# The shared expert and the router of a second transformer block, as products of split operands

## The chip, the core and the metric

The kernel runs on one core of a Trainium2 chip. Such a core has a matrix engine (TensorE, PE in the profile; its weight loads are PEld), a vector engine (VectorE, DVE), an activation engine (ScalarE, ACT), a general engine (GpSimd, POOL) and a queue engine (SyncE, SP). Each follows its own list of instructions in order; semaphores make one wait for another. SP and ACT also issue DMA transfers; those queues are SPq and ACTq in the profile. The metric is the time of one execution on the device in microseconds (us); less is better.

## The reference

Two transformer blocks, 512 tokens, model width 1024, all in float32. The second block is the one that matters here. It ends in

```python
    x = x + gate_m * hybrid_mixer(h, ...)                       # last product of the mixer: merged @ w_out
    h = rms_norm(x, g_ffn_norm[l]) * (1.0 + scale_f) + shift_f
    x = x + gate_f * moe_ffn(h, w_router, b_router, w_exp_gate, w_exp_up, w_exp_down,
                             w_sh_gate, w_sh_up, w_sh_down)
return rms_norm(x, g_final)
```

and `moe_ffn` is

```python
    scores = jax.nn.sigmoid(xf @ w_router)                      # 64 experts
    ...                                                         # 4 of 8 groups, then 6 experts per token
    shared = (jax.nn.silu(xf @ w_sh_gate) * (xf @ w_sh_up)) @ w_sh_down    # 1024 -> 256 -> 1024, every token
    return shared + routed
```

The rows `gate_m`, `scale_f`, `shift_f`, `gate_f` (1024 values each, one batch) come from a conditioning vector and are computed earlier in the kernel. The 64 routed experts have 3 MB of weights each.

## The kernel before

A tile is 128 partitions by so many elements; the 512 tokens are four tiles, t0 to t3. `xres` is the residual stream, tokens on partitions.

**Split operands.** Most dense products are made from operands in two parts. `hi` is the value copied to the type float32r, `lo` is the value minus `hi`, also float32r; `mm3` (lines 108 to 110) adds `hi*hi`, `lo*hi` and `hi*lo` in one PSUM bank. For weights `Kernel.weights` does it: it loads a chunk `w` of 128x1024 by SP's queue, ACT makes `wh` (line 136), and DVE or POOL makes `wl` (line 137). Both halves have two buffers, so a chunk's `wh` waits until PE is done with the chunk two before. The shared expert, the router and the routed experts use plain float32 products.

**Output projection (`finish` in `phase_c`).** `merged @ w_out` is made in two column halves, g = 0 and g = 1, each with four PSUM banks (one per token tile) and four weight chunks of 24 matmuls, 96 matmuls in all. Chunks 0 and 1 go over all four tiles; then each tile takes chunks 2 and 3 and is finished. Then DVE multiplies the bank with the gate row `gm` (line 1805) and adds it to `xres` (line 1806). The banks come from the pool `pj`, which has four:

```python
    def pbank(self, name="pbank"):
        return self.pj.tile([128, 512], F32, tag="p", name=name)
```

so the first matmul of g = 1 on t0 waits for the `xres` addition of g = 0 on t0.

**Head (`phase_d`).** Its loads are issued while `finish` runs: on ACT's queue the rows `scale_f` and `shift_f` (tile `rows`), `g_ffn_norm` and `gm` (the two halves of tile `gmr`), and, in the place of `g_ffn_norm` once that is used, the router's weights; on SP's queue the shared expert's weights (`sg` twice, `sd`) and the first expert weights. `rows` is completed by DVE at line 1852. For each tile, `head(t)` computes the norm, `logits(t)` makes `h`, writes it to DRAM (`hD`, from which the experts gather), transposes it (`xt`, 8 transposes), copies it to SBUF (`hT`) and multiplies with the router's weights (`lg`).

**Rest of the head (`rest_d`).** A sigmoid on the logits, the choice of experts on DVE (ending in `Ab`), counts, ranks and positions by small matmuls (`cnt`, `key`, `perm`, `pos`, `posT`, `posR`, `GT`, `Gr`, `ce`), then for each of the first units the chosen token numbers (`bc` on PE, `st`, `jk`, `ii` on DVE), the gather of their rows by POOL (`xg`) and of their gates (`gg`). Beside it PE computes the shared expert: `g` and `u` (64 instructions of 256 columns each), the hidden row on ACT and DVE, two transposes `hT`, `y` (32 instructions of 512 columns). DVE multiplies each `y` bank with the row `gf` (line 1005), and POOL adds it to `xres` (line 1974).

**Expert loop (`Moe.run`).** Units of routed experts follow, each: transposes `xT` of the gathered rows, `g`, `u`, `y`, and a scatter product `sc` added to `xres`. Weights come by SP's queue into 18 slots (15 + 2 + 1) shared with the head's own tiles; `O1` and `O2` say which group of slots the next tile takes, `F0` and `F1` how many units are fetched ahead, and `LP`, `RP` are priorities. The order on each engine is fixed at build time by a list scheduler that goes by program order, priorities and its own estimates.

Of the kernel before, what the change touches and what calls it, by code (L numbers as in the profile page):

```python
# [18 lines left out]
S, D = 512, 1024  # L19
# [35 lines left out]
class K:  # L55
# [611 lines left out]
LAST = 2  # L667

# [77 lines left out]
class Moe:  # L746
# [33 lines left out]
    def slot(self, shape, dt, name, hold=False, after=None):  # L780
# [713 lines left out]
def phase_c(k, rctx, rp, rows):  # L1494
# [293 lines left out]
    def finish(gm, done):  # L1788
        for g in range(2):
            gs_ = slice(512 * g, 512 * g + 512)  # L1790
            banks = [k.pbank("wo") for _ in range(NT)]
            ws = [k.weights(pw, [(I["w_out_2"][0], 512 * g, 512 * g + 512)], 2 * h, 2, 512, eng=nc.vector if WV[1] else None) for h in range(4)]
# [8 lines left out]
            for t in range(NT):  # L1801
# [3 lines left out]
                nc.vector.tensor_mul(b, b, gm[:, gs_])  # L1805
# [7 lines left out]
F0, F1 = 2, 3  # L1813
# [3 lines left out]
O1 = [0] * 3 + [1] * 2 + [0] * 12  # L1817
O2 = [0] * 3 + [1] * 2 + [2] + [0] * 12
# [6 lines left out]
def phase_d(k, out):  # L1825
# [19 lines left out]
    perm = f.tile([1, E], I32, name="perm")  # L1845
    rows_ = moe.slot([128, 2, D], F32, "rows")
# [7 lines left out]
    wr = gmr[:, 1, :KD * E].rearrange("p (k n) -> p k n", k=KD)  # L1854
    nc.scalar.dma_start(wr, I["w_router_2"][0].rearrange("(p k) n -> p k n", p=128))
# [23 lines left out]
    def logits(t):  # L1879
        lb, rs = lbs[0], rss[t]  # L1880
        ts = slice(t * 128, (t + 1) * 128)
        h, hT = h4[t // 2][:, t % 2], hTs[t]
        nc.vector.scalar_tensor_tensor(h, k.xres[:, t], rs, gs, op0=ALU.mult, op1=ALU.mult)
        nc.vector.tensor_add(h, h, sh)
        nc.scalar.dma_start(moe.hD[ts], h)
        for c in range(2):
# [3 lines left out]
            nc.scalar.activation(hT[:, 4 * c:4 * c + 4], b.rearrange("p (k s) -> p k s", k=4), AF.Copy)  # L1890
        for kk in range(KD):
            nc.tensor.matmul(lb[:, t * E:(t + 1) * E], lhsT=hT[:, kk], rhs=wr[:, kk], start=kk == 0, stop=kk == KD - 1)

    def rest():
        for t in range(NT - LL, NT):
            with tc.high_priority(LP):
                logits(t)
        moe.rooms()
        moe.work()
        rest_d(k, out, moe, lbs[0], br, f, perm, hTs, shared, ctx)  # L1900
# [3 lines left out]
def rest_d(k, out, moe, lb, br, f, perm, hTs, shared, ctx):  # L1904
# [62 lines left out]
    ws = [(128, shared)]  # L1967
    hTx = moe.m.tile([128, NT, 2, 128], F32, tag="xT", name="hTx", bufs=1)
    for t in range(NT):
        moe.hidden(hTs[t], ws, None, k.pbank, hT=hTx[:, t])  # L1970
    for t in range(NT):
        def add(h, b):
            xs = k.xres[:, t, h * 512:(h + 1) * 512]
            nc.gpsimd.tensor_add(xs, xs, moe.scaled(h, b, moe.m.tile([128, 512], F32, tag="yl", name="ysh", bufs=2)))
        moe.down(hTx[:, t], ws, add)
# [73 lines left out]
```

## Time and profile before

| | us |
|---|---|
| median of three runs (1662.69, 1664.47, 1668.43) | 1664.47 |
| the profiled execution | 1666.99 |
| its span | 1664.9 |
| PE busy in the span | 1543.6 |
| DVE / ACT / POOL busy | 968.7 / 540.6 / 341.9 |

The profiled execution lies 2.5 us above the median; 2.1 us of it lie outside the span. PE is busy for 93% of the span, and the chain of work that ended last runs on PE for 47% of the span and little on any other engine. Times in the text below are us from the start of the span. The second block's `finish` runs from 1009 to 1061, the head from there to 1126, the expert loop from 1126 to about 1650.

In a timeline each line is: start, duration, engine and source line, operation, output <- inputs, shapes, and in square brackets how long the engine was idle before and what released it. In groups of instructions it is: busy us, mean ns of one, then the idle time before them and its releaser. PEclk is the clock granted to PE as a share of 2.4 GHz.

### The profile page before, as it was taken

To read this page: it belongs to the slowest core of one execution; us is meant where nothing else is said; L and a number is where in the kernel's file an instruction comes from. 1 tells how busy PE (TensorE), PEld (TensorE's weight loads), DVE (VectorE), ACT (ScalarE), POOL (GpSimd) and SP (SyncE) were. 2 spreads that over 40 slices of the span, in tenths; PEclk is the share of its full clock that TensorE was granted. 3 is DMA by queue.
4 is the path that set the end of the run, shared out by engine and by line. 5 is a ranking of instruction groups with operands and counts; after the bars stand their busy time and mean duration, and the time that the engine had idled before them with its cause. 6 is when DMAs were issued, how large, how long until landed. Compare 5 with 4: busy or idle time off the path is not lost.

```text
span 1664.9 us, 28632 instructions
## 1 busy us (share of the span) xinstructions
PE 1543.6 (93%) x10917; PEld 1038.3 (62%) x10917; DVE 968.7 (58%) x2217; ACT 540.6 (32%) x1087; POOL 341.9 (21%) x285
## 2 busy tenths in 40 slices
PE   5899999988999877899999998999999999999996
PEld 4665557765565446675657776865666665665653
DVE  3599536853554347537554535555665666656656
ACT  4534676331211124555552222301211112112112
POOL 2324451012101103331104442022101111111000
PEclk9999999987999997999999999999999999999998
DMA  6443326368999963233005836758999999999961
GB/s 188 147 164 117 105 82 234 133 216 309 418 417 416 418 264 106 72 90 106 26 1 188 257 118 222 305 197 350 378 416 385 398 411 420 424 417 422 420 288 64
DMA packets 104783, 420.78 MB, mean 253 GB/s; under 512 B 23508, under 2 KB 30138, under 8 KB 67268
## 3 DMA queue, kind: packets, MB, share of 16 engines
q1 hardware_dynamic: 82880, 388.20, 60.7%
q0 software_dynamic: 9968, 19.04, 3.2%
q10 hardware_dynamic: 11796, 11.68, 2.2%
q8 instruction: 87, 1.43, 0.3%
q14 instruction: 52, 0.43, 0.1%
HBM read 419.99 MB, written 9.21 MB: 258 GB/s over the span
## 4 chain that ended last, share of the span: by engine, by line
PE 47%; DVE 4%; DMA 3%; POOL 1%; ACT 1%; issue 1%; SPq 0%; DVEq 0%; ACTq 0%; POOLq 0%
PE g L973 8%; PE u L973 7%; PE sc L1051 7%; PE y L997 7%; PE qk L1671 2%; PE ob L1699 2%; DMA mw<-in_w_mod_dram 2%; PE xT L938 2%; PE pt L110 2%; PE pt L109 2%; PE pt L108 2%; PE pt L1691 1%; DVE macc L1400 1%; DMA w<-in_w_in_dram 1%; PE wo L109 1%
## 5 line engine op out<-in xcount | busy, mean ns | idle before, releaser
L137 POOL TENSOR_TENSOR wl<-w,wh 128x1024 fp32r<-128x1024 f32 (+4 forms) x72 | 167.1, 2323 | 370.2 <-ACT wh L136 348.1
L1052 DVE TENSOR_TENSOR xres<-xres,sc 128x512 f32<-128x512 f32 x368 | 224.4, 681 | 3.4 <-PE sc L1051 1.0
L973 PE MATMUL u<-wu,xT 128*32 128x256 f32 (+2 forms) x2240 | 176.0, 388 | 11.2 <-DMA wu<-in_w_exp_up_dram 9.4
L973 PE MATMUL g<-wg,xT 128*32 128x256 f32 (+2 forms) x2240 | 173.6, 383 | 1.0 <-DMA wg<-in_w_exp_gate_dram 0.9
L915 POOL DMA_INDIRECT xg<-hD,ii x46 | 46.1, 1002 | 599.0 <-issue 500.7
L997 PE MATMUL y<-wd,hT 128*32 128x512 f32 (+2 forms) x1120 | 167.6, 596 | 0.0
L979 DVE SCALAR_TENSOR_TENSOR hid<-u,gc,hid 128x256 f32<-128x256 f32 x46 | 22.3, 484 | 232.8 <-PE u L973 227.7
L973 PEld LDWEIGHTS g<-wg,xT 128*32 128x32 f32 (+2 forms) x2240 | 99.2, 119 | 87.5 <-issue 31.5
L1051 PE MATMUL sc<-yh,st 128*128 128x512 f32 x368 | 152.2, 416 | 0.0
L973 PEld LDWEIGHTS u<-wu,xT 128*32 128x32 f32 (+2 forms) x2240 | 105.1, 121 | 73.0 <-DMA wu<-in_w_exp_up_dram 12.0
L136 ACT ACTIVATE wh<-w 128x1024 fp32r<-128x1024 f32 (+4 forms) x88 | 89.9, 1022 | 186.8 <-PE pt L109 85.3
L1051 PE MATMUL sc<-yl,st 128*128 128x512 f32 x368 | 144.4, 395 | 0.1
L987 ACT ACTIVATE hT<-hT 128x256 f32<-128x256 f32 x46 | 17.7, 385 | 299.5 <-PE hT L984 299.5
L116 ACT ACTIVATE yh<-y 128x512 fp32r<-128x512 f32 x92 | 54.9, 597 | 163.0 <-DVE y L1005 129.1
L108 PE MATMUL pr<-wh,xh 128*128 128x512 f32 (+2 forms) x256 | 101.9, 402 | 5.9 <-ACT wh L136 5.4
L109 PE MATMUL pr<-wl,xh 128*128 128x512 f32 (+2 forms) x256 | 101.2, 397 | 5.9 <-POOL wl L137 5.9
L997 PEld LDWEIGHTS y<-wd,hT 128*32 128x32 f32 (+2 forms) x1120 | 46.6, 118 | 90.7 <-issue 88.0
L117 DVE TENSOR_TENSOR yl<-y,yh 128x512 fp32r<-128x512 f32 x92 | 63.6, 692 | 67.1 <-ACT yh L116 66.7
L110 PE MATMUL pr<-wh,xl 128*128 128x512 f32 (+2 forms) x256 | 100.2, 395 | 0.2 <-DVE xl L117 0.2
L110 PE MATMUL pt<-xh,wl 128*128 128x512 f32 x224 | 90.1, 402 | 2.9 <-POOL wl L137 2.9
L108 PE MATMUL pt<-xh,wh 128*128 128x512 f32 x224 | 91.1, 407 | 0.5 <-ACT la L1570 0.3
L109 PE MATMUL pt<-xl,wh 128*128 128x512 f32 x224 | 89.8, 401 | 0.0
(532 smaller groups left out, 2802.6 us busy)
## 6 DMA issues: line engine op xcount, KB each, us to landing
wg<-in_w_exp_gate_dram SPq DMA_DIRECT2D x96, 1024.0 KB, 14.3
wu<-in_w_exp_up_dram SPq DMA_DIRECT2D x96, 1024.0 KB, 11.8
wd<-in_w_exp_down_dram SPq DMA_DIRECT2D x96, 1024.0 KB, 13.0
w<-in_w_in_dram SPq DMA_DIRECT2D x52, 512.0 KB, 3.7
mw<-in_w_mod_dram SPq DMA_DIRECT2D x32, 512.0 KB, 4.7
mw<-in_w_mod_dram SPq DMA_DIRECT2D x8, 1024.0 KB, 5.8
w<-in_w_out_dram SPq DMA_DIRECT2D x16, 512.0 KB, 4.5
brs<-brd ACTq DMA_DIRECT2D x1, 2560.0 KB
```

The costliest lines, as they stand in the source:

```text
L108: nc.tensor.matmul(out, lhsT=lh, rhs=rh, start=first, stop=False)
L109: nc.tensor.matmul(out, lhsT=lh, rhs=rl, start=False, stop=False)
L110: nc.tensor.matmul(out, lhsT=ll, rhs=rh, start=False, stop=last)
L116: hi = nc.scalar.activation(dh, src, AF.Copy)
L117: lo = nc.vector.tensor_sub(dl, src, dh.bitcast(F32))
L136: nc.scalar.activation(wh[:, :, :c], w[:, :, :c], AF.Copy)
L137: (eng or nc.gpsimd).tensor_sub(wl[:, :, :c], w[:, :, :c], wh[:, :, :c].bitcast(F32))
L915: self.gathered = nc.gpsimd.indirect_dma_start(out=x, out_offset=None, in_=src, in_offset=bass.IndirectOffsetOnAxis(ap=ii[:, :1], axis=0), ...
L973: nc.tensor.matmul(b[sl], lhsT=xT[:, kk, sl], rhs=g[h][:, kk], start=kk == 0, stop=kk == KD - 1)
L997: nc.tensor.matmul(b[sl], lhsT=hT[:, j, sl], rhs=d[:, j, h * 512:(h + 1) * 512], start=j == 0, stop=j == 1)
L1051: nc.tensor.matmul(b, lhsT=st[:, ts], rhs=y[h][i], start=i == 0, stop=i == 1)
L1052: nc.vector.tensor_add(self.acc[:, t, hs], self.acc[:, t, hs], b)
```

## The change

Five edits, all in the second block:

1. For g = 1 of the output projection, `gm` is multiplied into the weights (four times 128x1024 on DVE, new argument `times`), not onto the four banks.
2. The shared expert is made with `mm3`. Its weights are loaded as four 512 KB pieces (`sgu`, gate and up side by side) and `sd`, `gf` is multiplied into `sd`, and they are split (ACT `sgh` twice, `sdh`; DVE `sgl` twice, `sdl`); `y` is added to `xres` by DVE straight from the bank.
3. The router's weights stand as `hi` and `lo` side by side in 128 columns (`mid`); the transposed `h` is split too (`hh`, `hl`). Each pair of token tiles gets 16 matmuls of 256 columns. The bank holds two halves of rows that must be added: ACT copies it, and four float32 matmuls with a matrix `sum2` (two identities) add the halves and transpose (`lo`).
4. The first two units of the expert loop are prepared at high priority (`RUN`).
5. `F0` goes from 2 to 1, another fetch of 2 units follows, and `O1`, `O2` are changed for the new use of slots.

The core of the diff, cut:

```diff
-    def weights(self, pool, segs, k0, nk, width, wb=2, eng=None):
+    def weights(self, pool, segs, k0, nk, width, wb=2, eng=None, times=None):
...
+            if times is not None:
+                nc.vector.tensor_mul(w, w, times[:, None, :].to_broadcast([128, nk, width]))
...
+RUN = {32: 0, 64: 400}
...
-        for u in range(2):
-            self.pick(u)
-        self.prep(0)
-        with self.k.tc.issue_after(self.indexed.ins):
-            self.prep(1)
+        with self.k.tc.high_priority(RUN[self.E]):
+            for u in range(2):
+                self.pick(u)
+            self.prep(0)
+            with self.k.tc.issue_after(self.indexed.ins):
+                self.prep(1)
...
-            ws = [k.weights(pw, [(I["w_out_2"][0], 512 * g, 512 * g + 512)], 2 * h, 2, 512, eng=nc.vector if WV[1] else None) for h in range(4)]
+            ws = [k.weights(pw, [(I["w_out_2"][0], 512 * g, 512 * g + 512)], 2 * h, 2, 512, eng=nc.vector if WV[1] else None,
+                            times=gm[:, gs_] if g else None) for h in range(4)]
...
-                nc.vector.tensor_mul(b, b, gm[:, gs_])
+                if not g:
+                    nc.vector.tensor_mul(b, b, gm[:, gs_])
                 nc.vector.tensor_add(k.xres[:, t, gs_], k.xres[:, t, gs_], b)
...
-F0, F1 = 2, 3
+F0, F1 = 1, 3
...
-O1 = [0] * 3 + [1] * 2 + [0] * 12
-O2 = [0] * 3 + [1] * 2 + [2] + [0] * 12
+O1 = [0] * 16 + [1] * 2 + [0] * 6
+O2 = [2] + [0] * 6 + [1] * 2 + [0] * 9
...
+    sgu = [moe.slot([128, 4, 512], F32, "sgu") for _ in range(2)]
+    for q in range(2):
+        for c, n in enumerate(("w_sh_gate_2", "w_sh_up_2")):
+            nc.sync.dma_start(sgu[q][:, :, 256 * c:256 * c + 256],
+                              I[n][0].rearrange("(p k) f -> p k f", p=128)[:, 4 * q:4 * q + 4])
+    sd = moe.slot([128, 2, D], F32, "sd")
+    nc.sync.dma_start(sd, I["w_sh_down_2"][0].rearrange("(j p) n -> p j n", p=128))
...
+    nc.scalar.activation(wrp[:, :, :E], raw, AF.Copy)
+    nc.vector.tensor_sub(wrp[:, :, E:], raw, wrp[:, :, :E].bitcast(F32))
+    sum2 = gmr[:, 1, :E]
+    nc.vector.tensor_add(sum2, k.ident[:, :E], k.ident[:, E:])
+    for w, (wh, wl) in zip(sgu, sgu2):
+        nc.scalar.activation(wh, w, AF.Copy)
+        nc.vector.tensor_sub(wl, w, wh.bitcast(F32))
+    nc.vector.tensor_mul(sd, sd, gf[:, None, :].to_broadcast([128, 2, D]))
+    nc.scalar.activation(sdh, sd, AF.Copy)
+    sdl = part("sdl", (128, 2, D))
+    nc.vector.tensor_sub(sdl, sd, sdh.bitcast(F32))
...
-            nc.scalar.activation(hT[:, 4 * c:4 * c + 4], b.rearrange("p (k s) -> p k s", k=4), AF.Copy)
-        for kk in range(KD):
-            nc.tensor.matmul(lb[:, t * E:(t + 1) * E], lhsT=hT[:, kk], rhs=wr[:, kk], start=kk == 0, stop=kk == KD - 1)
+            k.split(hh[:, 4 * c:4 * c + 4, t % 2], hl[:, 4 * c:4 * c + 4, t % 2], b.rearrange("p (k s) -> p k s", k=4))
+        if t % 2 == 0:
+            return
...
+        nc.tensor.matmul(o, lhsT=wrp[:, 0], rhs=both(hh, 0), start=True, stop=False)
+        for kk in range(KD):
+            nc.tensor.matmul(o[:E], lhsT=wrp[:, kk, :E], rhs=both(hl, kk), start=False, stop=False)
+        for kk in range(1, KD):
+            nc.tensor.matmul(o, lhsT=wrp[:, kk], rhs=both(hh, kk), start=False, stop=kk == KD - 1)
...
+            nc.scalar.activation(pt, lbs[0], AF.Copy)
+            for t in range(NT):
+                nc.tensor.matmul(lb[:, t * E:(t + 1) * E], lhsT=pt[:, t * 128:(t + 1) * 128], rhs=sum2, start=True, stop=True)
...
-            nc.gpsimd.tensor_add(xs, xs, moe.scaled(h, b, moe.m.tile([128, 512], F32, tag="yl", name="ysh", bufs=2)))
+                k.mm3(b, mh[:, t, j], ml[:, t, j], sdh[:, j, cs], sdl[:, j, cs], j == 0, j == 1)
+            nc.vector.tensor_add(k.xres[:, t, cs], k.xres[:, t, cs], b)
```

How the instructions stand is told by the order on two engines. The first place is DVE at the change from the first column half of the output projection to the second. Before, from the `wl` of the third chunk on (`wl` is the low part of a chunk, `wo` a bank, `gmr` the tile that holds `gm`):

```order
L137 TENSOR_TENSOR wl<-w,wh 128x1024
L1852 SCALAR_TENSOR_TENSOR rows<-rows,gmr 128x1024
L137 TENSOR_TENSOR wl<-w,wh 128x1024
L1805 TENSOR_TENSOR wo<-wo,gmr 128x512
L1806 TENSOR_TENSOR xres<-xres,wo 128x512
L1805 TENSOR_TENSOR wo<-wo,gmr 128x512
L1806 TENSOR_TENSOR xres<-xres,wo 128x512
L1805 TENSOR_TENSOR wo<-wo,gmr 128x512
L1806 TENSOR_TENSOR xres<-xres,wo 128x512
L137 TENSOR_TENSOR wl<-w,wh 128x1024
```

Now, from behind the `wl` of the fourth chunk on (`w<-w,gmr` is the gate row times a chunk, `mid` the router's low part, `gmr<-ident` is `sum2`; `sgl` and `sdl` are the shared expert's low parts):

```order
L1879 TENSOR_TENSOR sd<-sd,gf 128x2048
L1855 SCALAR_TENSOR_TENSOR rows<-rows,gmr 128x1024
L135 TENSOR_TENSOR w<-w,gmr 128x1024 x2
L1801 TENSOR_TENSOR wo<-wo,gmr 128x512
L139 TENSOR_TENSOR wl<-w,wh 128x1024 x2
L1873 TENSOR_TENSOR mid<-gmr,mid 128x8x64
L1878 TENSOR_TENSOR sgl<-sgu,sgh 128x2048
L135 TENSOR_TENSOR w<-w,gmr 128x1024 x2
L1875 TENSOR_TENSOR gmr<-ident 128x64
L1878 TENSOR_TENSOR sgl<-sgu,sgh 128x2048
L1882 TENSOR_TENSOR sdl<-sd,sdh 128x2048
L1802 TENSOR_TENSOR xres<-xres,wo 128x512
```

Before, the completion of `rows` stands ahead of the fourth chunk's `wl`, and each bank's addition to `xres` follows its multiplication at once. Now the fourth chunk comes first; `sd`, `rows` and two weight chunks stand ahead of the first bank's multiplication, and seven rows (nine instructions) of other work between it and that bank's addition.

The second place is ACT at the same time, where its DMA issues stand among the copies (`wh` is the high part of a chunk, `xh` the high part of the projection's input). Before:

```order
L1774 ACTIVATE xh<-tb_8736 128x512 x2
L1848 DMA rows<-modD 128x2048
L136 ACTIVATE wh<-w 128x1024
L1851 DMA gmr<-in_g_ffn_norm_dram 128x1024
L1853 DMA gmr<-modD 128x1024
L136 ACTIVATE wh<-w 128x1024
L1855 DMA gmr<-in_w_router_dram 128x512
L136 ACTIVATE wh<-w 128x1024 x4
```

Now:

```order
L1768 ACTIVATE xh<-tb_8736 128x512 x2
L138 ACTIVATE wh<-w 128x1024 x2
L1851 DMA rows<-modD 128x2048
L1854 DMA gmr<-in_g_ffn_norm_dram 128x1024
L1856 DMA gmr<-modD 128x1024
L1858 DMA gmr<-in_w_router_dram 128x512
L138 ACTIVATE wh<-w 128x1024 x2
L1872 ACTIVATE mid<-gmr 128x8x64
L1877 ACTIVATE sgh<-sgu 128x2048 x2
L1880 ACTIVATE sdh<-sd 128x2048
```

The loads of `rows`, of `g_ffn_norm` and of `gm` have moved from ahead of the third and fourth chunk's `wh` to behind the fourth's, and the splits of router and shared expert stand ahead of the `wh` of the last two chunks.

## Rows read from the trace of the kernel before

**Rows 1.** Windows: stretch, busy us (x instructions) of PE, PEld, DVE, ACT, POOL; PEclk, DMA share, GB/s.

```profile
1018.00:1023.00 5.00, 5.00 (x22) 3.68 (x21) 0.00 (x0) 1.06 (x1) 0.00 (x0) 1.00 1.04 410
1038.20:1061.00 22.80, 22.50 (x97) 17.65 (x96) 12.17 (x20) 5.78 (x9) 0.28 (x3) 1.00 0.86 338
1061.00:1125.60 64.60, 61.17 (x316) 46.00 (x315) 38.45 (x113) 14.81 (x28) 14.76 (x16) 1.00 0.56 205
1125.60:1651.00 525.40, 522.92 (x4968) 319.11 (x4968) 328.06 (x704) 102.46 (x202) 65.56 (x66) 1.00 0.92 376
```

**Rows 2.** Waits of SP's DMA queue, 1126 to 1652: total us, times, longest.

```profile
SPq L802 <- PE y L997: 222.5, 30, 8.0
```

**Rows 3.** Waits of PE, 1000 to 1126: total us, times, longest.

```profile
PE wo L109 <- DVE wl L137: 4.5, 2, 4.2
```

**Rows 4.** Timeline of PE, first column half: start, us, what, [idle before <- releaser].

```profile
1018.72 0.39 PE L110 MATMUL wo<-wh,xl 128*128 128x512 f32 x1
1021.44 0.39 PE L110 MATMUL wo<-wh,xl 128*128 128x512 f32 x1
1022.65 0.39 PE L108 MATMUL wo<-wh,xh 128*128 128x512 f32 x1
1027.23 0.79 PE L109 MATMUL wo<-wl,xh 128*128 128x512 f32 x1 [4.19 <-DVE wl L137]
1027.82 0.63 PE L110 MATMUL wo<-wh,xl 128*128 128x512 f32 x1
1031.66 0.63 PE L108 MATMUL wo<-wh,xh 128*128 128x512 f32 x1
```

**Rows 5.** Timeline of ACT and its DMA queue, 1014 to 1027.

```profile
1014.10 0.33 ACTq L1848 DMA_DIRECT2D rows<-modD  x1
1015.07 0.33 ACTq L1851 DMA_DIRECT2D gmr<-in_g_ffn_norm_dram  x1
1020.50 1.06 ACT L136 ACTIVATE wh<-w 128x1024 fp32r<-128x1024 f32 x1 [4.38 <-PE wo L110]
1026.07 0.33 ACTq L1855 DMA_DIRECT2D gmr<-in_w_router_dram  x1
```

**Rows 6.** Timeline of DVE, 1024 to 1028.

```profile
1024.81 1.23 DVE L1852 SCALAR_TENSOR_TENSOR rows<-rows,gmr 128x1024 f32<-128x1024 f32 x1 [7.43 <-DMA gmr<-in_g_ffn_norm_dram]
1025.95 1.22 DVE L137 TENSOR_TENSOR wl<-w,wh 128x1024 fp32r<-128x1024 f32 x1
```

**Rows 7.** Groups of PE instructions, 1061 to 1126: busy, mean ns, idle before.

```profile
L1892 PE MATMUL lg<-gmr,hT 128*128 128x64 f32 x64 | 8.0, 271 | 1.2 <-ACT hT L1890 1.2
```

**Rows 8.** Groups of DVE instructions, 1000 to 1126.

```profile
L1005 DVE TENSOR_TENSOR ysh<-y,gf 128x512 f32<-128x512 f32 x8 | 5.5, 690 | 3.8 <-POOL xres L1974 2.5 <-PE y L997 1.3
L1884 DVE TENSOR_TENSOR h<-h,rows 128x1024 f32<-128x1024 f32 x4 | 4.9, 1220 | 0.0
```

**Rows 9.** Groups of ACT instructions, 1000 to 1126.

```profile
L136 ACT ACTIVATE wh<-w 128x1024 fp32r<-128x1024 f32 x8 | 8.5, 1059 | 30.2 <-PE wo L110 29.9 <-PE pt L109 0.3
```

**Rows 10.** Timeline of all engines, from routing's end to the first expert unit.

```profile
1105.83 3.62 PE L973 MATMUL u<-sg,hT 128*128 128x256 f32 x16
1110.38 13.90 PE L997 MATMUL y<-sd,hTx 128*128 128x512 f32 x32
1111.59 0.14 DVE L913 TENSOR_SCALAR ii<-ix 128x1 int32<-128x1 f32 x1
1112.53 1.09 POOL L915 DMA_INDIRECT xg<-hD,ii  x1 [49.13 <-DVE st L906]
1115.10 1.04 POOL L915 DMA_INDIRECT gg<-gD,ii  x1 [0.17 <-POOL xres L1974]
1119.18 0.47 DVE L948 COPY gc<-gg 64x1 f32<-64x1 f32 x3 [2.69 <-DMA gg<-gD,ii]
1124.11 1.05 PE L938 MATMUL xT<-ident,xg 128*128 128x128 f32 x8
1125.63 1.07 PE L973 MATMUL g<-wg,xT 128*32 128x256 f32 x16
```

More of the change, by code (lines that the diff above doesn't have):

```diff
@@ L1858, in phase_d, with part @@
     h4 = [moe.slot([128, 2, D], F32, "h4", True) for _ in range(2)]
-    hT4 = [moe.slot([128, 2, KD, 128], F32, "hT4", True) for _ in range(2)]
-    hTs = [hT4[t // 2][:, t % 2] for t in range(NT)]
-    shared = moe.load_from(I["w_sh_gate_2"][0], I["w_sh_up_2"][0], I["w_sh_down_2"][0])
+    def part(n, shape=(128, 4, 512), hold=False):
+        return moe.slot(list(shape), F32R, n, hold)
+    rows4 = (128, KD, 2, 128)
+    hs = [[part(n, rows4, True)] for n in ("hh", "hl")]
+    sgu2 = [[part(n) for n in ("sgh", "sgl")] for _ in range(2)]
+    sdh = part("sdh", (128, 2, D))
+    mid = part("mid")
+    wrp = mid[:, :2].rearrange("p a (k n) -> p (a k) n", n=128)
+    nc.scalar.activation(wrp[:, :, :E], raw, AF.Copy)
[9 more added lines that the diff above has]
+    nc.vector.tensor_sub(sdl, sd, sdh.bitcast(F32))
+    for c, n in zip(hs, ("hh", "hl")):
+        c.append(part(n, rows4, True))
     moe.fetch(F0, 0)
@@ L1897, in rest, with rest_d @@
                 logits(t)
+        lb = k.bank("lo")
+        with tc.high_priority(LP):
+            pt = gmr[:, 1, 512:]
+            nc.scalar.activation(pt, lbs[0], AF.Copy)
+            for t in range(NT):
+                nc.tensor.matmul(lb[:, t * E:(t + 1) * E], lhsT=pt[:, t * 128:(t + 1) * 128], rhs=sum2, start=True, stop=True)
         moe.rooms()
         moe.work()
-        rest_d(k, out, moe, lbs[0], br, f, perm, hTs, shared, ctx)
+        moe.fetch(2, 0)
+        rest_d(k, out, moe, lb, br, f, perm, hs, (sgu2, sdh, sdl, mid), ctx)
     return gm, head, rest
-def rest_d(k, out, moe, lb, br, f, perm, hTs, shared, ctx):
+def rest_d(k, out, moe, lb, br, f, perm, hs, shared, ctx):
     nc, tc, I = k.nc, k.tc, k.I
@@ L1964, in rest_d @@
     moe.ranked(Gt, p, f)
-    ws = [(128, shared)]
-    hTx = moe.m.tile([128, NT, 2, 128], F32, tag="xT", name="hTx", bufs=1)
+    sgu, sdh, sdl, mid = shared
+    mh = moe.m.tile([128, NT, 2, 128], F32R, tag="xT", name="mh", bufs=1)
+    ml = mid[:, 2:].rearrange("p a (b s) -> p a b s", s=128).rearrange("p a (c j) s -> p (a c) j s", j=2)
     for t in range(NT):
-        moe.hidden(hTs[t], ws, None, k.pbank, hT=hTx[:, t])
-    for t in range(NT):
-        def add(h, b):
-            xs = k.xres[:, t, h * 512:(h + 1) * 512]
-            nc.gpsimd.tensor_add(xs, xs, moe.scaled(h, b, moe.m.tile([128, 512], F32, tag="yl", name="ysh", bufs=2)))
-        moe.down(hTx[:, t], ws, add)
+        b = k.pbank("gu")
+        for kk in range(KD):
+            wh, wl = [w[:, kk % 4] for w in sgu[kk // 4]]
+            k.mm3(b, *[x[t // 2][:, kk, t % 2] for x in hs], wh, wl, kk == 0, kk == KD - 1)
+        hid = moe.m.tile([128, 256], F32, tag="hid", name="hid", bufs=1)
+        nc.scalar.activation(hid, b[:, :256], AF.Silu)
+        nc.vector.tensor_mul(hid, b[:, 256:], hid)
+        b = k.bank("hT")
+        for j in range(2):
+            nc.tensor.transpose(b[:, j * 128:(j + 1) * 128], hid[:, j * 128:(j + 1) * 128], k.ident)
+        k.split(mh[:, t], ml[:, t], b[:, :256].rearrange("p (j s) -> p j s", j=2))
+    for t in range(NT):
+        for h in range(2):
+            cs = slice(512 * h, 512 * h + 512)
+            b = k.pbank("y")
+            for j in range(2):
+                k.mm3(b, mh[:, t, j], ml[:, t, j], sdh[:, j, cs], sdl[:, j, cs], j == 0, j == 1)
+            nc.vector.tensor_add(k.xres[:, t, cs], k.xres[:, t, cs], b)
     moe.run()
```

20 lines of the change are left out of this document (8 added, 12 removed).

## The prediction

> **What bounds the kernel now.** I read the page's chain first, then windows over the second block, then the waits of PE and of SP's queue, then timelines of the two places the change touches. The reader is to see three things. In the expert loop PE is busy for 522.92 of 525.40 us [rows 1], and SP's queue waits for PE there, 222.5 us for the `y` products alone [rows 2]: weights lie ready and PE sets the pace. The change leaves the loop's products alone, so it moves the end only by moving the loop's start, 1125.6. In the head ahead of it PE is busy for 61.17 of 64.6 us [rows 1]: work taken from PE there counts almost wholly. In the output projection PE had one wait of weight: of its 4.5 us behind `wl`, 4.19 are one stop at 1023.0 [rows 3, 4]. So the sum has three terms: first column half, second column half, head.
>
> **First half.** The stop comes from DVE: ahead of the fourth chunk's `wl` stands the completion of `rows`, which waited 7.43 us for `g_ffn_norm` [rows 6]. Now that `wl` comes first. Its `wh` starts at 1020.50, held by PE's use of the buffer two chunks before [rows 5], so it stays there: 1020.50 + 1.06 + 1.22 = 1022.8, and PE arrives at 1022.65 + 0.39 = 1023.0 [rows 4]. The 4.2 us go. After the stop PE worked at the lower clock: from 1027.82 to 1031.66, nine matmuls at 0.43 each, where the twelve from 1018.72 to 1021.44 took 0.227 each [rows 4]. With the two ahead of these and one behind, that is twelve slow ones, 12 x 0.2 = 2.4 us, which go too. The half ends at 1038.2 - 6.6 = 1031.6.
>
> **Second half.** Its first matmul on t0 takes the bank of the first half's t0 and waits until DVE has added that to `xres`. Before, that addition followed the bank's multiplication at once. Now DVE has, in this order: `sd*gf`, `rows`, two gated chunks, the bank's multiplication, two `wl`, `mid`, `sgl`, two more gated chunks, `sum2`, `sgl`, `sdl`, and only then the addition. Behind it wait all of PE's work and, on SP's queue, the first expert weights.
>
> When does this chain start? `rows` waits for loads that ACT now issues behind the fourth `wh`: `rows` at 1021.6 where it was 1014.10, `g_ffn_norm` 0.97 later as before, 1022.5 [rows 5]. The same load took 1024.81 - 1015.07 = 9.7 us before [rows 5, 6], while the DMA engines moved 410 GB/s [rows 1]; a small transfer, the gather of gates, was there 4.1 us after its issue at 1115.10 (1119.18) [rows 10]. So it lands between 1026.6 and 1032.2. The traffic ahead of it is mostly the same but has a few us more to drain; I take 7.3 us, nearer to the row of the same load: 1029.8. `rows` takes 1.22, and the gated chunks start at 1031.0 (bounds 1027.8 to 1033.4).
>
> From there DVE has six pieces of 128x1024 at 1.14 spacing (1024.81 to 1025.95 [rows 6]), that is two gated, two `wl`, two gated, 6.8; three pieces of 128x2048, which no row shows, taken as two pieces of 1.14 each, 6.8; three of 128x512 (`wo`, `mid`, `xres`) at 0.69 [rows 8], 2.1; `sum2` 0.1: 15.8. The larger pieces are bounded by one and by two of 1.22 [rows 8], 12.5 to 16.4 in all. The first `sgl` also waits for ACT, which copies `mid` only after the router's load, issued behind `rows`, has landed, and then `sgh`, two pieces of 1.06 [rows 9]: 0.5 us more. PE starts again at 1031.0 + 16.3 = 1047.3, after 15.7 us of nothing, where before it went on at once.
>
> The half itself took 22.8 us [rows 1]. After an idle stretch of 4.2 us the clock was low for twelve matmuls; after this longer one I take the same 2.4 us, with 0 and 5 as bounds. It ends at 1047.3 + 22.8 + 2.4 = 1072.5, against 1061.0: **+11.5 us**, of which the first half's gain of 6.6 is already taken off. From the bounds: +5 to +17. The four bank multiplications that go from the half's end (0.69 each, one on the path) save 0.7, counted in the head.
>
> The Trainium skill, page "DMA: Bandwidth & Descriptors", section "Measured (HBM→SBUF, 128 partitions, SWDGE, issued from GpSimd)", says to batch transfers to 1 MiB or more, which reach 341 GB/s alone. It speaks against the four 512 KB loads that stand where two of 1 MB stood. By it the 4 MB or so in the air would take 2 us longer than at 410 GB/s and the chain would start that much later (an estimate); the window from 1018 to 1023 has several transfers of both sizes at once and disagrees.
>
> **Head.** PE's work: `u` of one tile took 3.62 us for 16 instructions [rows 10], some 3.45 from start to start, so `g` and `u` together 8 x 3.45 = 27.6, and `y` 13.9 [rows 10], 41.5 in all. Now there are 96 + 48 = 144 matmuls of 512 columns at 0.227 [rows 4], 32.7: -8.8. The router took 8.0 us [rows 7]. Now 32 matmuls of 256 columns at half of 0.227, 3.6, and four float32 ones of 64 columns, each two of that row's 64 records at 8.0/64, 1.0: -3.4. Together -12.2.
>
> What of it reaches the end? The loop cannot start before the gathered rows are there. `ii` was ready at 1111.59, 50.6 us after the projection's end; the gather was issued 0.94 later [rows 10]; with the landing of 4.1, `xT` could have begun at 1116.6, but PE was still in `y` until 1124.1. With PE free 12 us earlier the gather ends last: `xT` at 55.7 after the projection's end, the loop 1.5 later (1124.11 to 1125.63 [rows 10]), 57.2. The way to `ii` changes little: the bank multiplication (-0.7) and shorter router products (-1) against the subtraction for `hl` (+0.7), the copy of the bank (+0.6) and the four matmuls `lo` (+1.0), while DVE loses eight multiplications and gains eight additions, eight `hl` and four `ml` of at most 0.69, beside PE's work. I take -0.6. The loop starts 56.6 after the projection's end, where it was 64.6: **-8.0**. The bounds are -12.2, PE's whole gain, and -3, if the additions that DVE now makes between `st`, `jk` and `ii` and the weights that load during the gather hold it up by 5 us.
>
> **Loop and the rest.** The shared expert's parts now hold slots for longer, so fewer expert weights are there when the loop starts. The six 1 MB pieces of the first unit are asked for between the splits (1044) and the logits; at 376 GB/s [rows 1] they take 16.7 us and are there some 30 us before the loop. Later ones follow as slots come free. I put 0, with +6 as the other end. POOL's additions go, off the path. `F0`, `O1`, `O2` and `RUN` only set this order; nothing of their own.
>
> **Sum.** 11.5 - 8.0 = +3.5 on the profiled execution of 1666.99, which stands 2.5 above the median: 1664.47 + 3.5 = **1668.0 us**.
>
> **The rivals.**
> - *The bank wait costs nothing much.* If the data land early and DVE is through its chain by the time PE ends the first half, the second half runs from 1031.6, ends at 1054.4, 6.6 earlier, and with -8.0 the kernel takes 1649.9. For it speaks that only one DVE row forces the wait; against it that 12.5 us of DVE work stand behind a load that cannot be there before 1026.6. Half of it, a low end of every bound, is 5 - 8 = -3, or with the whole gain in the head -7: 1657.
> - *The loop starves.* The shared parts' slots are freed by the last `gu` and `y` products; if the second unit's weights wait for them, PE waits in the first units. Decisive is whether a unit's 6 MB, 16 us at 376 GB/s, are asked for 16 us before use. Price 6: 1674.
> - *The gains in the head don't come.* The gather, next to loads of weights, lands as late as PE used to be free: -3 instead of -8, with +11.5 this is 1673. For it speaks that the loads now fall into the gather's time; against it that the 4.1 us were measured in a stretch that moved 205 GB/s on the mean [rows 1], so beside other loads too.
> - *The splitting buys nothing*, if products of 256 columns or 128 rows cost as before: against it stands the projection's own 0.227.
>
> **How the numbers follow.** The forecast has 0.55, its own range 1664 to 1672; the early rival and its half 0.15, starving 0.12, the head without gain 0.15, the last 0.03. About 0.3%, 5 us, is what a measurement of this kernel can tell from no change. Of the forecast 0.38 lie within 5 us, 0.13 above and 0.04 below; the early rival gives 0.13 to faster and 0.02 to same; the others 0.25 to slower and 0.05 to same. That makes faster 0.17, same 0.45, slower 0.38. For 8 in 10 the range reaches from the half of the early rival, 1657, to a full chain with one of the later costs, 1677.
>
> **What would show it.** Right: no stop behind `wl` in the first half; one idle stretch of PE of 12 to 19 us between the halves, released by DVE's `xres` addition, low clock behind it; `y` done ahead of the gather, and `xT` released by the gather's DMA; a loop of 525 us. Wrong: PE idle under 8 us between the halves, waits for `wg`, `wu` or `wd` of over 2 us in the loop, or a head that still takes over 61 us.

## The result, and the profile after

The changed kernel takes 1677.44 us (median of nine runs, 1674.35 to 1686.15), the kernel before on the same chip 1667.56 (nine runs, 1662.69 to 1674.13). The ratio is 1.0066, 95% interval 1.005 to 1.0082: slower by 10 us by the medians, 11 by the ratio. The profiled execution has a span of 1677.3.

Windows of the changed kernel follow (columns as in [rows 1]): first column half, bank wait, second half, the head's first 12 us, the rest of the head, the loop.

```profile
1012.00:1034.50 22.50, 22.50 (x98) 17.79 (x96) 10.31 (x10) 4.85 (x6) 4.12 (x6) 1.00 0.81 300
1034.50:1052.80 18.30, 0.01 (x1) 0.01 (x1) 17.44 (x16) 8.04 (x6) 0.00 (x0) 0.63 0.36 116
1052.80:1077.90 25.10, 25.03 (x104) 19.74 (x104) 12.62 (x25) 6.55 (x12) 0.72 (x3) 0.93 0.17 71
1077.90:1090.00 12.10, 6.96 (x38) 6.33 (x38) 12.04 (x28) 4.34 (x9) 2.16 (x4) 0.72 0.74 261
1090.00:1137.00 47.00, 45.14 (x226) 34.82 (x225) 29.49 (x90) 7.49 (x15) 4.11 (x4) 0.96 0.74 277
1137.00:1664.00 527.00, 523.90 (x4974) 319.70 (x4972) 329.26 (x706) 104.40 (x205) 63.81 (x64) 1.00 0.92 379
```

PE does nothing for 18.3 us between the halves, while DVE works for 17.44 of them. At the head's start the same engine is busy for 12.04 of 12.10 us and PE for 6.96. PE's waits from the projection to the loop (columns as in [rows 3]) name the releasers:

```profile
PE wo L108 <- DVE xres L1802: 18.3, 1, 18.3
PE xt L1913 <- DVE h L1907: 5.1, 1, 5.1
PE xT L931 <- DMA xg<-hD,ii: 0.7, 1, 0.7
```

The wait behind `wl` of [rows 3] is gone; in its place stands the predicted one. From the starts of the projection's first product, its end, the first expert's `g` and the span's end (before 1009.30, 1061.03, 1125.63, 1664.9; now 1012.23, 1077.92, 1137.88, 1677.3):

| us | before | after | change | predicted |
|---|---|---|---|---|
| first half | 28.9 | 22.3 | -6.6 | -6.6 |
| PE idle between the halves | 0 | 18.3 | +18.3 | +15.7 |
| second half | 22.8 | 25.1 | +2.3 | +2.4 |
| head | 64.6 | 60.0 | -4.6 | -8.0 |
| loop and end | 539.3 | 539.4 | +0.1 | 0 |
| sum | | | +9.5 | +3.5 |

The profiled span grew by 12.4. The other 2.9 lie ahead of the projection, in code that the change leaves alone; in the profiles below its first product starts anywhere from 1005.7 to 1015.0.

DVE between the halves, in the changed kernel's timeline; it answers to [rows 6]:

```profile
1024.50 1.22 DVE L139 TENSOR_TENSOR wl<-w,wh 128x1024 fp32r<-128x1024 f32 x1 [4.21 <-ACT wh L138]
1032.87 2.29 DVE L1879 TENSOR_TENSOR sd<-sd,gf 128x2048 f32<-128x2048 f32 x1 [7.14 <-DMA sd<-in_w_sh_down_dram]
1035.08 1.22 DVE L1855 SCALAR_TENSOR_TENSOR rows<-rows,gmr 128x1024 f32<-128x1024 f32 x1
1036.21 2.35 DVE L135 TENSOR_TENSOR w<-w,gmr 128x1024 f32<-128x1024 f32 x2
1038.48 0.69 DVE L1801 TENSOR_TENSOR wo<-wo,gmr 128x512 f32<-128x512 f32 x1
...
1049.80 2.28 DVE L1882 TENSOR_TENSOR sdl<-sd,sdh 128x2048 fp32r<-128x2048 f32 x1
1052.00 0.68 DVE L1802 TENSOR_TENSOR xres<-xres,wo 128x512 f32<-128x512 f32 x1
```

DVE stands for 7.14 us, but for `sd`'s load, not for `g_ffn_norm` as in [rows 6]: `rows` follows without a wait. The bank's multiplication ends at 1039.1 and its addition begins at 1052.00: 12.9 us of the wait lie between the two, in the nine instructions that now stand there. SP's and ACT's queues of the same timeline show when the two were issued, in place of [rows 5]:

```profile
1021.26 0.50 SPq L1848 DMA_DIRECT2D sd<-in_w_sh_down_dram  x1
1023.79 0.44 ACTq L1854 DMA_DIRECT2D gmr<-in_g_ffn_norm_dram  x1
```

The 1 MB of `sd` took 11.6 us (1021.26 to 1032.87). PE behind the wait, in place of [rows 4]:

```profile
1052.82 0.77 PE L108 MATMUL wo<-wh,xh 128*128 128x512 f32 x1 [18.32 <-DVE xres L1802]
1053.38 0.63 PE L109 MATMUL wo<-wl,xh 128*128 128x512 f32 x1
...
1056.40 0.41 PE L109 MATMUL wo<-wl,xh 128*128 128x512 f32 x1
1056.65 0.39 PE L110 MATMUL wo<-wh,xl 128*128 128x512 f32 x1
...
1076.64 1.13 PE L1913 MATMUL xt<-ident,h 128*128 128x128 f32 x8
```

From the restart to 1056.40 eight products take 3.58 us, most of them 0.43 apart, at the lower of the two clocks; then they stand 0.23 apart. The transposes of t0 now lie inside the half. The end of the head, all engines, answers to [rows 10]:

```profile
1109.48 0.42 DVE L1995 TENSOR_TENSOR Ab<-cv 128x256 bf16<-128x256 f32 x1
...
1120.18 0.27 PE L856 MATMUL ce<-cv 64*64 64x2 f32 x2
...
1122.32 0.63 PE L110 MATMUL y<-sdh,mid 128*128 128x512 f32 x1
1122.74 0.63 PE L108 MATMUL y<-sdh,mh 128*128 128x512 f32 x1
...
1127.93 0.72 PE L896 MATMUL bc<-posT,sel 128*128 128x512 f32 x2
1130.76 0.15 DVE L906 TENSOR_SCALAR ii<-ix 128x1 int32<-128x1 f32 x1
1131.71 1.09 POOL L908 DMA_INDIRECT xg<-hD,ii  x1 [51.42 <-DVE st L899]
1135.13 0.40 PE L110 MATMUL y<-sdh,mid 128*128 128x512 f32 x1
1136.27 1.13 PE L931 MATMUL xT<-ident,xg 128*128 128x128 f32 x8 [0.74 <-DMA xg<-hD,ii]
1137.88 1.50 PE L966 MATMUL g<-wg,xT 128*32 128x256 f32 x23
```

`y` ends ahead of the gather and the gather releases `xT`, as forecast; but `ii` comes 52.8 us after the projection's end where it came after 50.6. The kernel before had, in the same places:

```profile
1092.46 0.43 DVE L1955 TENSOR_TENSOR Ab<-cv 128x256 bf16<-128x256 f32 x1
...
1102.93 0.27 PE L863 MATMUL ce<-cv 64*64 64x2 f32 x2
...
1109.09 0.82 PE L903 MATMUL bc<-posT,sel 128*128 128x512 f32 x2
```

### The profile page after: what moved, and what is told of

It is laid out like the page before. It is cut to its first block, busy times and chain, and to the rows that moved or that the text cites. A ratio compares the mean times of both kernels' runs of the same rounds, so it can differ in the third digit from the quotient of the medians.

```text
span 1677.3 us, 28574 instructions
## 1 busy us (share of the span) xinstructions
PE 1538.2 (92%) x10877; PEld 1037.6 (62%) x10877; DVE 984.6 (59%) x2235; ACT 546.0 (33%) x1091; POOL 332.6 (20%) x279
## 4 chain that ended last, share of the span: by engine, by line
PE 48%; DVE 4%; DMA 3%; POOL 1%; ACT 1%; issue 1%; SPq 0%; DVEq 0%; ACTq 0%; POOLq 0%
PE sc L1044 7%; PE g L966 7%; PE y L990 7%; PE u L966 7%; PE qk L1665 2%; PE ob L1693 2%; PE pt L110 2%; PE pt L108 2%; PE pt L109 2%; PE xT L931 2%; DMA mw<-in_w_mod_dram 1%; PE pt L1685 1%; DMA w<-in_w_out_dram 1%; DVE macc L1394 1%; PE wo L108 1%; DMA w<-in_w_in_dram 1%
## 5 line engine op out<-in xcount | busy, mean ns | idle before, releaser
L972 DVE SCALAR_TENSOR_TENSOR hid<-u,gc,hid 128x256 f32<-128x256 f32 x46 | 22.3, 484 | 234.7 <-PE u L966 234.7
L966 PEld LDWEIGHTS u<-wu,xT 128*32 128x32 f32 (+2 forms) x2240 | 105.2, 122 | 75.0 <-DMA wu<-in_w_exp_up_dram 11.8
## 6 DMA issues: line engine op xcount, KB each, us to landing
wg<-in_w_exp_gate_dram SPq DMA_DIRECT2D x96, 1024.0 KB, 14.3
```

Source lines behind the costliest of these rows:

```text
L966: nc.tensor.matmul(b[sl], lhsT=xT[:, kk, sl], rhs=g[h][:, kk], start=kk == 0, stop=kk == KD - 1)
```

## The experiments

All ratios are to the kernel before, run beside them on the same chip. The experiments come from three chips, so lengths out of two profiles agree less well than ratios. "Finish" is the time from the projection's first product to the start of its last, "head" from there to the first expert's `g`: 51.3 and 65.0 before, 65.3 and 60.35 changed.

### The wait between the halves

**Other banks.** The second half takes its banks from the other pool, so it need not wait for the additions:

```diff
-            banks = [k.pbank("wo") for _ in range(NT)]
+            banks = [(k.bank if g else k.pbank)("wo") for _ in range(NT)]
```

> The changed kernel, but the second column half of the output projection takes its four banks from the other PSUM pool, so that its first matmul waits for no addition to xres. Theory (the bank wait is the loss): PE no longer waits for the xres addition at 1052 but only for the gated chunk's low part, which DVE had ready 10.6 us earlier (1041.4 in the changed kernel); the idle stretch between the halves falls from 18.3 to 6 to 8 us, and the kernel is 8 to 11 us faster than the changed one, 0 to 3 us slower than before. Rival (the late loads or the splits themselves are the loss, the bank is only the last of several waits): PE stops again at the next bank or low part, and less than 4 us come back.

Ratio 0.9983 [0.9968, 0.9997], 0.83% under the changed kernel, some 14 us. Finish 51.0, head 62.7. PE's waits there:

```profile
PE xt L1913 <- DVE two L1098: 5.9, 1, 5.9
PE wo L108 <- ACT wh L138: 4.4, 1, 4.4
PE xt L1913 <- DVE rs1y L91: 2.1, 1, 2.1
PE xT L931 <- DMA xg<-hD,ii: 1.3, 1, 1.3
```

The bank is the cause of the wait: 18.3 us become 4.4, now for the next chunk's `wh`, and more comes back than the theory had (6 to 8 us left, 8 to 11 gained). The head is 2.4 longer, mainly in its waits for DVE (5.9 and 2.1 where one of 5.1 was).

**Addition first.** Edit 1 undone (`times=None`, all four banks of the second half multiplied again), the first half's multiplication and addition at high priority:

```diff
-                if not g:
+                with tc.high_priority(0 if g else 900):
                     nc.vector.tensor_mul(b, b, gm[:, gs_])
-                nc.vector.tensor_add(k.xres[:, t, gs_], k.xres[:, t, gs_], b)
+                    nc.vector.tensor_add(k.xres[:, t, gs_], k.xres[:, t, gs_], b)
```

> The changed kernel with the gate row multiplied onto the banks in both halves (edit 1 undone) and the first half's bank multiplications and xres additions at high priority, so that they stand ahead of the splits on DVE. Theory: PE starts the second half 2 us after DVE has completed rows (1036.3 in the changed kernel), waits 1 to 4 us once more for a low part behind the eight additions, and the idle stretch falls from 18.3 to 5 to 9 us; the kernel is 9 to 13 us faster than the changed one, that is -2 to +2 us from before. Rival (the head lost by the splits being late): the splits now stand behind the additions, the shared expert's and the router's parts are ready later, and what the projection gains the head gives back: 0 to 4 us faster than the changed one.

Ratio 1.0012 [0.9997, 1.0027]; finish 53.1, head 60.9. With the same banks and DVE's order changed, 4.8 us of waiting for `xres` are left (longest 3.8), at the low end of the theory's 5 to 9. Both ways out of the wait work; that this one also takes the gated chunks out of DVE's list is not tested apart. The loop began with a wait of 3.5 us for DVE's `rw`, and the span behind the first `g` was 4.8 longer.

**Edit 1 alone**, put into the kernel before (the diff's lines with `times` and `if not g`):

> The kernel before with edit 1 alone (gate row into the weights of the second half). Theory: four multiplications of 128x1024 stand on DVE where four of 128x512 stood, DVE has the room, the path to the head is 0.7 us shorter: -1 to +1 us from before. Rival (edit 1 is a good part of the loss, since the low part of each chunk now waits for the gate row's load and a multiplication): +3 to +6 us.

Ratio 1.0009 [0.9996, 1.0022]; finish 53.2, and the wait behind `wl` of 4.2 stands as in [rows 3]. Gating weights instead of banks makes no long wait by itself. With 12.9 of the 18.3 us between the bank's multiplication and its addition, and 4.8 left when the addition comes first, most of the wait is the nine instructions of other work there.

**`sd` later.** Its multiplication and split are issued behind the first half's additions, so that `rows` need not stand behind `sd`'s load (cut):

```diff
+        with tc.issue_after(k.added):
+            nc.vector.tensor_mul(sd, sd, gf[:, None, :].to_broadcast([128, 2, D]))
+            nc.scalar.activation(sdh, sd, AF.Copy)
+            nc.vector.tensor_sub(sdl, sd, sdh.bitcast(F32))
```

> The changed kernel with the three operations on sd (times gf, high part, low part) held back until the first half's last addition to xres. Theory (the chain in front of the bank's addition is late because it begins with sd, whose 1 MB landed 11.6 us after its issue, later than the rows): two pieces of 2.3 us leave the chain, and rows starts when g_ffn_norm is there, 0 to 3 us before sd was; the idle stretch of 18.3 falls to 11 to 14 us, and the kernel is 4 to 7 us faster than the changed one, 4 to 7 above before. Rival (rows and gm land as late as sd): the stretch falls by the 4.6 us of DVE work alone or less, and as sd is split in the head it costs there: 0 to 3 us faster than the changed one.

Ratio 1.0067 [1.0046, 1.0087], no gain, less than theory or rival had; PE still waits 18.1 us, and the head took 63.3, 3.0 more. DVE's timeline of this kernel shows why:

```profile
1029.87 1.23 DVE L1857 SCALAR_TENSOR_TENSOR rows<-rows,gmr 128x1024 f32<-128x1024 f32 x1 [7.88 <-DMA gmr<-in_g_ffn_norm_dram]
1031.91 2.36 DVE L135 TENSOR_TENSOR w<-w,gmr 128x1024 f32<-128x1024 f32 x2 [0.82 <-DMA gmr<-modD]
...
1041.01 1.23 DVE L135 TENSOR_TENSOR w<-w,gmr 128x1024 f32<-128x1024 f32 x1 [1.06 <-DMA w<-in_w_out_dram]
1044.49 1.23 DVE L135 TENSOR_TENSOR w<-w,gmr 128x1024 f32<-128x1024 f32 x1 [2.26 <-DMA w<-in_w_out_dram]
1047.97 0.68 DVE L1802 TENSOR_TENSOR xres<-xres,wo 128x512 f32<-128x512 f32 x1
```

`rows` came 21.4 us after the projection's start instead of 22.9, without `sd` ahead of it; what that and the absent `sdl` gave was lost to loads of `gm` and of the last two weight chunks (0.82 + 1.06 + 2.26, where the changed kernel has one such wait, 0.80). DVE's chain is held by loads at several places, and with one gone the next is late.

**Other banks, `sd` later, edit 1 undone**, three of the edits above:

> The changed kernel with other banks for the second half, sd held back until the first half's last addition, and the gate row multiplied onto the banks in both halves. Theory: the second half waits only for the fourth chunk's low part behind rows, one pair of bank multiplications and one addition; the idle stretch is 1 to 4 us (4.4 with other banks alone), the head as with other banks alone: 2 to 5 us faster than before. Rival (what the projection gains the head gives back, since sd is split beside the logits): as with other banks alone or slower, 0 to 3 us faster than before.

Ratio 0.9983 [0.9966, 0.9999], as with other banks alone, as the rival had it: the finish fell to 50.3, the head rose to 64.2, with waits of 5.5 and 2.9 for DVE at its start.

### The head

**Priority of the first units as before:**

```diff
-RUN = {32: 0, 64: 400}
+RUN = {32: 0, 64: 0}
```

> The changed kernel without the high priority of the first units' preparation (edit 4 undone). Theory: it only sets an order in the head, the gather and the loop's start move by less than 2 us, the time stays within 2 us of the changed kernel, 10 to 12 us above before. Rival (the preparation put ahead of the shared expert is what the head lost): 4 us or more faster than the changed one.

Ratio 1.0101 [1.0083, 1.012]: 0.35% more than the changed kernel, some 6 us, where theory and rival had it equal or faster. `bc` stood behind all of `y`, `xT` waited 10.4 us for the gather, and the head took 69.4. The prediction had put this edit at nothing; without it the head would be longer than before.

**PE's wait filled.** Twenty products whose result nothing uses, in the 5.1 us that PE waits for `h` (cut):

```diff
+        if t == 1:
+            b = k.bank("fill")
+            with tc.issue_after(k.turned):
+                for j in range(20):
+                    nc.tensor.matmul(b, lhsT=wrp[:, 0], rhs=sgu2[0][0][:, 0], start=j == 0, stop=j == 20 - 1)
```

> The changed kernel with 20 matmuls of 128x512 (split weights of router and shared expert, result used by nothing) put on PE between the transposes of t0 and of t1 in the head, where PE waited 5.1 us for h of t1. Theory (the head lost part of its gain to that wait and to the low clock behind it): the matmuls take 20 x 0.23 = 4.6 us of a time in which PE did nothing, xt of t1 starts when it did, and the stretch behind it, granted 0.71 over 6.8 us, runs at 1.00: some 2 us less, head 58.4 instead of 60.35, time about 1675.5, ratio to the kernel before 1.005. Rival A (DVE's h, hl and xres set the pace there, PE's clock is of no matter): head 60.3, ratio 1.0066. Rival B (the added matmuls are in the way): head 61 to 64, ratio over 1.007. The wait of 18 us in the projection stays in all cases.

Ratio 1.0073 [1.005, 1.0095]; the head took 60.36, as without them. The same stretch as the fourth window above, of this kernel:

```profile
1080.60:1092.70 12.10, 10.22 (x59) 8.39 (x58) 12.10 (x27) 4.12 (x9) 2.14 (x4) 1.00 0.67 244
```

The granted clock is 1.00 where it was 0.72, and nothing is won. DVE has no free moment there: rival A. PE's low clock in this stretch is a consequence, not a cost. (The two heads are from single profiles; that they agree to 0.01 us is chance.)

**The router tile by tile** instead of by pairs of tiles (cut):

```diff
-        if t % 2 == 0:
-            return
-        o = lb[:, t // 2 * 256:t // 2 * 256 + 256]
+        o = lb[:, t * 128:(t + 1) * 128]
```

> The changed kernel with the router's products made tile by tile (128 columns) and not by pairs of tiles (256 columns). Theory (the head's gain fell short because PE has nothing to do until a pair is complete, waits 5.1 us for h of t1 and then runs at the lower clock): PE works on t0's logits in that time, the wait falls to 1 to 3 us, the head takes 57.5 to 59 us from the projection's last matmul to the first expert matmul where it took 60.3; 1 to 3 us faster than the changed one, 8 to 10 above before. Rival (the logits' chain on DVE and ACT sets the routing, the idle PE costs nothing): the wait falls, the head stays within 1 us of 60.3.

Ratio 1.0051 [1.0032, 1.0071], within the interval of the changed kernel; head 59.2, PE's wait 2.9. A us in the head, which the times can't tell; and it does not come by way of that wait, for `Ab` stands 0.8 us later after the start of the projection's last product (32.73 against 31.95). What is shorter is the stretch ahead of `bc`: the same seven `hT` and 19 `y` take 5.99 us at a granted clock of 1.00, against 7.48 at 0.77.

**The choice first**, with other banks: the code of `bc`, `st`, `jk`, `ii` and the gathers written ahead of the shared expert (cut; `begin` holds the lines of edit 4).

```diff
     moe.ranked(Gt, p, f)
+    moe.begin()
```

> Other banks, and the first two units' token choice (bc, st, jk, ii and the gathers) written ahead of the shared expert instead of behind it, so that bc stands on PE right behind the routing's last product and ahead of all y. With other banks alone the head took 62.7 us and xT waited 1.3 us for the gather. Theory (the head ends with the routing's chain and the gather, and bc stood some 7 us too late behind hT and y): ii comes 5 to 8 us earlier after the projection's end, xT waits for nothing, and PE's own work sets the loop's start: head 61 to 61.5, ratio about 0.9975, not more, since PE is then late by its own work and its earlier wait for h. Rival A (the gather is no bound): ii earlier, head unchanged at 62.7. Rival B: the shared expert's hidden rows, which share a buffer with jk, come later, and PE waits for them: head 63 to 66, ratio 0.999 or more.

Ratio 1.0045 [1.0029, 1.0062], 0.6% above other banks alone. `ii` came 47.2 us after the start of the projection's last product instead of 54.1, and `xT` waits for nothing; yet the head takes 74.0, beyond rival B's 63 to 66. From DVE's and PE's timelines of this kernel:

```profile
1104.77 0.15 DVE L906 TENSOR_SCALAR ii<-ix 128x1 int32<-128x1 f32 x1
...
1108.69 0.66 PE L2024 MATMUL hT<-ident,hid 128*128 128x128 f32 x2 [3.62 <-DVE hid L2021]
...
1115.72 0.47 DVE L941 COPY gc<-gg 64x1 f32<-64x1 f32 x3 [7.17 <-DMA gg<-gD,ii]
1116.21 0.42 DVE L117 TENSOR_TENSOR mid<-hT,mh 128x256 fp32r<-128x256 f32 x1
1116.69 0.80 PE L110 MATMUL y<-sdh,mid 128*128 128x512 f32 x1 [5.58 <-DVE mid L117]
...
1130.09 1.05 PE L931 MATMUL xT<-ident,xg 128*128 128x128 f32 x8
```

Rival B, and one thing more than it said: besides the 3.6 us for the shared buffer, `gc` now stands ahead of the shared expert's `mid` on DVE and waits there 7.17 us for the gates' gather. PE's two waits, 3.62 and 5.58, are most of the 11.3 us by which the head is longer; from 1112 to 1131 its granted clock was 0.77.

### Together

Other banks with the filled wait:

> The same 20 matmuls, with the second column half's banks taken from the other pool. Without the matmuls that kernel took 1666.1 (ratio 0.9983) and its head 62.7, with waits of 2.1 and 5.9 us before the transposes of t0 and t1 and a granted clock of 0.55 from 7 to 15 us after the projection's end. Theory: the wait of 5.9 is filled for 4.6, the low clock behind it goes, 8 us at 0.55 become some 5: head 59 to 60, ratio about 0.9965. Rival A (DVE sets the pace): head 62.7, ratio 0.998. Rival B (in the way): head 64 or more, ratio over 0.999.

Ratio 0.9976 [0.9962, 0.999], head 61.8: the wait of 5.9 is gone, and 0.9 us of the 2.7 to 3.7 that the theory had came of it.

Other banks with the router tile by tile:

> Other banks and the router's products tile by tile (32 matmuls of 128 columns and the rest likewise, instead of pairs of tiles); the loads and sd as in the changed kernel. Tile by tile alone had made the head 1.15 us shorter; other banks alone were 14 us faster than the changed kernel. If the two add up: head 61.5, finish 51, ratio 0.9975. If the head only waits for DVE: 62.7, ratio 0.998. If, as with sd moved, what one gains the head gives back: head 64 to 66, ratio 0.9985 or more.

Ratio 0.9963 [0.9942, 0.9983], head 62.65, as long as with other banks alone. `Ab` stands 1.7 us earlier, but the stretch ahead of `bc` takes 8.55 at a granted clock of 0.62 instead of 5.82 at 1.00.

Other banks, `sd` later, edit 1 undone, and the router tile by tile:

> The kernel of e7 with the router's products tile by tile. Theory: the gains add up, the projection as in e7 and the head 1 to 3 us shorter: 4 to 8 us faster than before. Rival (the gather ends last in any case and follows the chain on DVE): within 1 us of e7.

Ratio 0.9986 [0.997, 1.0002], finish 48.8 (the shortest), head 65.8: what the finish gains the head gives back, as the rival had it. The five kernels with other banks and the choice left in its place have overlapping intervals, from 0.9963 to 0.9986. Any of them beats the changed kernel, and four of them, by up to 0.4%, the kernel before; which is best can't be told.

## Why the prediction was wrong

Of the 9.4 us between 1668.0 and 1677.44, 3.1 are the base and no part of the mechanism: nine runs of the kernel before have a median of 1667.56, the three it went by 1664.47. By the profiles, nearly all of the rest is two terms of the sum, the wait for the bank (2.6 too short) and the head (3.4 too short): +3.5 was forecast and +9.5 came. All that the prediction named as a sign of being right came, and none of its signs of being wrong: the path was right, two sizes on it were not.

- **First half: right.** It is 6.6 shorter, by the stop and the slow products behind it.
- **The bank wait: mechanism right, start mis-sized.** The gated chunks began 24.0 us after the projection's first product (1036.21 - 1012.23), the forecast was 21.7. The step that failed is "when does this chain start": it let `rows` begin when `g_ffn_norm` lands, 20.5, and put `sd*gf`, first in its own list, at nothing ahead of that. `sd*gf` has a load of its own, which landed at 20.6, and its 2.2 us came on top; that is the 2.3.
- **What luck hid in this wait.** That `g_ffn_norm` landed within 1 us of the forecast (21.4, with `sd` later) was luck: it was issued 1.6 us earlier, beside the fourth `wh` and not behind it, and took 9.8 us and not 7.3. Behind the start of the gated chunks the chain took 16.6 us to PE's restart, forecast 16.3. That is the pieces as added up (those of 128x2048 cost 2.29 each, two of 1.14, as taken), without the 0.5 for ACT, and with 0.80 for a weight chunk's load that was not in the sum. Added again, the bounds of the pieces are 12.7 and 16.3 and not 12.5 and 16.4, and the low end of the whole term is between +2 and +3, not +5.
- **The estimate by the smaller loads: not the reason.** The prediction's estimate from the Trainium skill, page "DMA: Bandwidth & Descriptors", section "Measured (HBM→SBUF, 128 partitions, SWDGE, issued from GpSimd)", was a start 2 us later, at the 341 GB/s that 1 MiB transfers reach alone. The start did slip 2.3, but not for that reason: while `sd` loaded, 408 GB/s were moved.
- **Low clock behind it: right in sum**, 2.3 for 2.4, by luck in part: only some 1.7 of it is the clock (eight products in 3.58 us, 8 x 0.23 = 1.84 at the other clock); the rest are t0's eight transposes, which moved here from the head.
- **Head: the way to `ii` mis-sized.** Forecast -0.6, measured +2.3 (52.8 against 50.6). The parts named (-0.7, -1, +0.7, +0.6, +1.0) add up to +0.6, not -0.6; they all lie ahead of `Ab`, and the way to `Ab` came out at +0.1 (31.56 against 31.43 from the projection's end). Most of what was missed lies behind it: 1.8 between `Ab` and `bc` (18.45 against 16.63), of which 1.6 behind `ce`, where PE made the first of the `y` at the lower clock (0.43 apart), a term that the prediction put at nothing there. From `ce`'s end to `bc` it took 7.5 us for seven `hT` and 19 of the 48 `y`, where 5.9 of `g` and `u` stood before:

```profile
1120.40:1128.00 7.60, 7.13 (x28) 5.37 (x27) 4.38 (x14) 2.08 (x6) 0.00 (x0) 0.78 1.01 420
```

  The same products in the same place took 6.0 us in three of the experiments (addition first; the router tile by tile; other banks, `sd` later, edit 1 undone), at a granted clock of 1.00, and 7.4 to 8.6 in four others, at 0.77 to 0.62. So at the higher clock the queue ahead of `bc` costs what it did before; the clock is what was missed. In the changed kernel PE had waited 0.65 us for `cv` and 0.47 for `mh` just ahead of it; what decides between the two levels is not shown. Then 0.3 were lost between `bc` and `ii`, and the gather took 4.56 us to `xT`, not 4.1. Together 3.4. The rival without gain in the head had the gather's landing as its cause; that is 0.5 of it.
- **DVE's additions "beside PE's work": not so in the head's first 12 us.** DVE has no gap there, and filling PE's time changed nothing, so what lies there, the first `hl` among it, is not hidden. The prediction shows no row for DVE's room in this stretch. DVE was nearly full there already, as one window of the kernel before shows, and only its mean over the whole head (38.45 of 64.6 us, [rows 1]) looks free. By the +0.1 to `Ab` the price was small:

```profile
1061.00:1073.10 12.10, 10.30 (x76) 9.69 (x76) 11.43 (x30) 5.74 (x13) 2.40 (x5) 1.00 0.56 196
```

- **"Nothing of their own" for `RUN`: wrong.** It is worth some 6 us; the gain in the head depends on it.
- **Loop: right**, +0.1; weights did not starve it, and the rivals that cost it something didn't come.

What stays open: in seven of the kernels (`sd` later in all three forms, the tiles in both others, the filled wait in both) the time behind the first `g` was 543 to 547 us instead of 539 to 540, mostly with PE busy and waiting for nothing. These seven all ran on one chip, the other experiments on two others, and the kernel before, run beside the seven, had medians of 1673.4 and 1674.0 instead of 1667.5 to 1668.2. So the difference goes with the runs on that chip and not with the edits, which is why only the ratios are compared; what makes it is not known. (With the addition first the same stretch took 544.1 on another chip; 3.5 of that are its wait for `rw`.)

## What to carry over

When edits put work on an engine between "bank read" and "bank released", price the wait from the loads that this engine must see in its order: every instruction ahead that has a load begins no earlier than that load lands, and its own time comes on top. Or give the next user another bank if one is free. Where a chain of small steps sets a stage's end, follow the chain through each engine's queue, and ask at which clock what stands ahead of it will run: work removed from the busiest engine counts only as far as it stood ahead of the chain's own instructions. Gains found one at a time here did not add up, since each shifted the wait to the next late load or to the same busy engine a stage later.

## What was not expected of the hardware

- A 1 MB load landed 11.6 us after its issue, though 408 GB/s were moved in that time, longer than the 9.7 us of 512 KB in [rows 5, 6]. The page of the kernel before had a row for such loads: its expert weights, 1 MB each, took 11.8 to 14.3 us in the median (operation, count, KB each, us from issue to landing):

```profile
wg<-in_w_exp_gate_dram SPq DMA_DIRECT2D x96, 1024.0 KB, 14.3
```

- After 18.3 us without work PE ran eight products at the lower clock, and after the 4.2 us of [rows 4] twelve: the longer rest did not make the slow stretch longer.
- The granted clock over 12 us went from 0.72 to 1.00 with work that served only to fill, and the head took as long as before (60.35 and 60.36). Later in the same head, ahead of `bc`, the lower clock cost 1.5 us: there the path ran on PE.
